# Mixing stage: two projection tiles that follow each other share one buffer of raw weights

## The chip, the cores and the metric

The kernel runs on one core of one Trainium2 chip. The metric is device time in microseconds (us): three runs of the kernel before took 1103.85, 1106.62 and 1107.76 us, and their median, 1106.62, is the time before. The core has five engines that each work through their own instructions in order: TensorE (PE: matmuls; its weight loads are listed apart as PEld), VectorE (DVE), ScalarE (ACT), GpSimd (POOL) and SyncE (SP), which here only issues transfers from device memory. Engines wait for each other and for transfers by semaphores.

## The reference

One step of a hybrid decoder layer on 512 new prompt tokens and 8 sequences of 4 new tokens each, 544 tokens in all, with a model width of 1024. A half-step SwiGLU feed-forward network comes first, then the mixing stage, then a second feed-forward network. What the mixing stage computes, cut down:

```python
proj = h @ w_in                       # h: normed tokens, w_in: 1024 x 3592
q_a, k_a, v_a, q_m, k_m, v_m, o_m, gates = jnp.split(proj, idx, axis=-1)
# 4 heads of differential attention, per query block of 128:
logits = einsum('bqhcd,bkhcd->bchqk', q, k) * ATT_DQ ** -0.5   # c = 2 halves of 64
p = softmax(where(mask, logits + bias, -inf)); a = p[:, 0] - lam * p[:, 1]
attn = a @ v                          # the 8 sequences also attend to paged caches
# 4 heads of chunkwise mLSTM on q_m, k_m, v_m with the gates, and its new states
h_m = rmsnorm(h_m) * sigmoid(o_m)
return concat([attn, h_m]) @ w_out, k_rows, v_a, C, n, m
```

Everything is float32.

## The kernel before, in words

**Matmuls.** The 544 tokens are worked on in two halves of 272 columns. A float32 matrix product is made of three passes over numbers that are rounded to a shorter format (`mm3`, L253 to L255): high weights times high tokens, high weights times low tokens, low weights times high tokens. The tokens are split into high and low once; the weights are split on the chip, tile by tile, in `parts`: ScalarE casts the raw weights to the high part `wh` (L241), and VectorE subtracts that from the raw weights to get the low part `wl` (L242).

**Weights of the mixing stage.** `w_in` without its gates is 28 tiles of 128 columns, each 1024 x 128 float32, 512 KB. A tile is loaded by the sync queue (L226, in `load_raw`) into a raw buffer, [128, 8, 256] float32, and only the first 128 of its 256 columns are used. The raw buffers are two (L854), and the split parts wh and wl have three buffers each (L855). A tile's split is two casts of 128 x 512 and two subtractions. `mix_weights` (L1662) is a generator: each `next` on it issues one tile's load and split. The tiles come in the order 0, 4, 8, 1, 2, 3, 5, 9, 6, 10, 7, 11 (query, key and value of the four attention heads), then 12, 16, 20, 13, ... (the mLSTM heads) and 24 to 27 (output gates). The gates' weights and tiles 0 and 4 are asked for early, at the end of the feed-forward network (`next_h`, L829); the others when `mix` (L1673) projects with them.

**What else runs in the stage.** `mix` interleaves the projections with side work: the gate work of the mLSTM (`gates`, L1091 to L1200: small ScalarE and VectorE instructions in a long chain, some of whose results TensorE needs at L1160 and L1183), attention blocks (`attn_block`, L1298) and the attention to the paged caches (`attn_samples`: gathers on GpSimd's queue, L1360, transposed by TensorE at L1386). An attention head starts with `key_parts` (cs, L1283 and L1284) and `query_parts` (vb, L1293 and L1295): ScalarE casts and VectorE subtracts, and TensorE's logits matmul (L1311) needs both. There is one buffer vb, so the parts of the next query block are made after the logits of this one.

**What sets the order.** All of this is written as Python generators. A tile scheduler then decides, when the kernel is built, the order in which each engine holds its instructions, by program order, by its own estimates of time and by when buffers come free; on the chip that order is fixed. A change in where a load is issued can therefore move instructions of other engines.

Of the kernel before, what the change touches and what calls it, by code (L numbers as in the profile page):

```python
# [10 lines left out]
F32 = mybir.dt.float32  # L11
# [19 lines left out]
H = 4  # L31
# [3 lines left out]
KT = D // 128  # L35
# [170 lines left out]
class _Builder:  # L206
# [1000 lines left out]
        nc.vector.tensor_copy(out=self.ncol, in_=ps[:, 0:NS])  # L1207


    def w_in_tile(self, mt):  # L1210
        win = self.i["w_in"][0].rearrange("(k p) m -> p k m", p=128)
        return self.split(self.load_raw(win[:, :, mt * 128:mt * 128 + 128], 128), KT, 0)

    def proj_half(self, w, hs, dst, half, scale):
        ps = self.acc_tile(half)
# [446 lines left out]
    def mix_weights(self):  # L1662

        yield self.gate_weights()
        for mt in [0, 4, 8, 1, 2, 3] + [4 * a + h for h in range(1, H) for a in (1, 2)]:
            yield self.w_in_tile(mt)
        for h in range(H):
            for a in range(3):
                yield self.w_in_tile(12 + 4 * a + h)
        for h in range(H):  # L1670
            yield self.w_in_tile(24 + h)

    def mix(self, hs, ws, gpost, finish, before):  # L1673
        nc, tc = self.nc, self.tc
# [336 lines left out]
```

## Time and profile before

| what | value |
| --- | --- |
| median of three runs | 1106.62 us |
| span of the profiled execution (its own time; no other is listed for it) | 1109.2 us |
| mixing stage in that span | about 345 to 712 us |
| TensorE busy | 1088.8 us, 98% |
| ScalarE's casts of raw weights (128 x 512 and two other forms) | 165 instructions, 126.8 us |
| VectorE's subtractions for them | 165 instructions, 146.9 us |
| loads of w_in tiles | 28 of 512 KB, 4.8 us (median) from issue to landing |

In the rows of a timeline the columns are the start in us from the start of the span, the duration, the engine, the line, the operation with its tiles (out<-in) and shapes, how many instructions the row holds, and in brackets the idle time of the engine ahead of it and what ended that. A matmul's duration includes time in which the next has started already; the distance between two starts tells the pace. "The granted clock" is the share of full speed that TensorE was given.

### The profile page before, as it was taken

To read this page: it belongs to the slowest core of one execution; us is meant where nothing else is said; L and a number is where in the kernel's file an instruction comes from. 1 tells how busy PE (TensorE), PEld (TensorE's weight loads), DVE (VectorE), ACT (ScalarE), POOL (GpSimd) and SP (SyncE) were. 2 spreads that over 40 slices of the span, in tenths; PEclk is the share of its full clock that TensorE was granted. 3 is DMA by queue.
4 is the path that set the end of the run, shared out by engine and by line. 5 is a ranking of instruction groups with operands and counts; after the bars stand their busy time and mean duration, and the time that the engine had idled before them with its cause. 6 is when DMAs were issued, how large, how long until landed. Compare 5 with 4: busy or idle time off the path is not lost. (4 is left out here: it accounts for less than half of the span.)

```text
span 1109.2 us, 21539 instructions
## 1 busy us (share of the span) xinstructions
PE 1088.8 (98%) x8610; PEld 1050.2 (95%) x8610; DVE 855.4 (77%) x1626; ACT 639.5 (58%) x1288; POOL 163.2 (15%) x212
## 2 busy tenths in 40 slices
PE   9999999999999999999999999999999999999997
PEld 8999999999999998899789888999999999999997
DVE  5898787887677898668666477799978778957865
ACT  6554544565567756666545466675555455555664
POOL 3100000001210424320333442001000000012000
PEclk9999999999999999999999999999999999999999
DMA  9723233237994346533345545864223323299832
GB/s 265 252 94 114 81 111 115 76 96 208 223 245 128 93 121 172 175 112 82 103 148 160 178 136 177 248 216 161 89 87 105 114 77 106 67 270 206 191 97 81
DMA packets 145588, 160.33 MB, mean 145 GB/s; under 512 B 6013, under 2 KB 135397, under 8 KB 144208
## 3 DMA queue, kind: packets, MB, share of 16 engines
q1 hardware_dynamic: 115008, 99.05, 29.5%
q0 software_dynamic: 27472, 57.14, 20.8%
q10 hardware_dynamic: 3008, 2.78, 0.9%
q8 instruction: 67, 1.10, 0.4%
q14 instruction: 33, 0.27, 0.1%
HBM read 143.19 MB, written 16.28 MB: 144 GB/s over the span
## 5 line engine op out<-in xcount | busy, mean ns | idle before, releaser
L241 ACT CAST wh<-raw 128x512 fp32r<-128x512 f32 (+2 forms) x165 | 126.8, 795 | 97.3 <-PE acc L254 34.3
L242 DVE TENSOR_TENSOR wl<-raw,wh 128x512 fp32r<-128x512 f32 (+2 forms) x165 | 146.9, 904 | 43.4 <-ACT wh L241 42.7
L253 PE MATMUL acc<-h,wh 128*128 128x272 f32 x552 | 165.7, 300 | 0.0
L255 PE MATMUL acc<-h,wl 128*128 128x272 f32 x552 | 161.4, 293 | 0.0
L254 PE MATMUL acc<-h,wh 128*128 128x272 f32 x552 | 161.0, 292 | 0.0
L483 PE MATMUL acc<-t,wh 128*128 128x272 f32 x472 | 136.7, 290 | 0.0
L485 PE MATMUL acc<-t,wl 128*128 128x272 f32 x472 | 136.5, 290 | 0.0
L484 PE MATMUL acc<-t,wh 128*128 128x272 f32 x472 | 136.1, 289 | 0.0
L253 PEld LDWEIGHTS acc<-h,wh 128*128 128x128 f32 x552 | 104.9, 190 | 8.1 <-issue 7.5
L255 PEld LDWEIGHTS acc<-h,wl 128*128 128x128 f32 x552 | 104.9, 190 | 0.6 <-issue 0.4
L254 PEld LDWEIGHTS acc<-h,wh 128*128 128x128 f32 x552 | 105.1, 190 | 0.3 <-DVE y L1459 0.2
L483 PE MATMUL acc<-h,wh 128*128 128x272 f32 x360 | 104.2, 290 | 0.0
L485 PE MATMUL acc<-h,wl 128*128 128x272 f32 x360 | 104.2, 289 | 0.0
L484 PE MATMUL acc<-h,wh 128*128 128x272 f32 x360 | 103.6, 288 | 0.0
L242 DVE TENSOR_TENSOR wl<-X,wh 128x1024 fp32r<-128x1024 f32 x66 | 80.7, 1223 | 28.3 <-ACT wh L241 28.3
L241 ACT CAST wh<-X 128x1024 fp32r<-128x1024 f32 x66 | 69.3, 1050 | 40.6 <-PE aux L484 26.0
L484 PEld LDWEIGHTS acc<-t,wh 128*128 128x128 f32 x472 | 89.0, 189 | 0.0
L483 PEld LDWEIGHTS acc<-t,wh 128*128 128x128 f32 x472 | 88.8, 188 | 0.0
L485 PEld LDWEIGHTS acc<-t,wl 128*128 128x128 f32 x472 | 88.7, 188 | 0.1
L732 POOL DMA_DIRECT2D late<-in_ffn_w_down_dram x12 | 18.8, 1563 | 439.4 <-DVE wl L242 241.6
L485 PE MATMUL aux<-h,wl 128*128 128x272 f32 x240 | 69.6, 290 | 0.4 <-DVE wl L242 0.4
L483 PE MATMUL aux<-h,wh 128*128 128x272 f32 x240 | 69.4, 289 | 0.0
(522 smaller groups left out, 3288.6 us busy)
## 6 DMA issues: line engine op xcount, KB each, us to landing
raw<-in_ffn_w_gate_dram SPq DMA_DIRECT2D x18, 1024.0 KB, 5.8
raw<-in_w_in_dram SPq DMA_DIRECT2D x28, 512.0 KB, 4.8
late<-in_ffn_w_down_dram POOLq DMA_DIRECT2D x12, 1024.0 KB
rawx<-in_ffn_w_up_dram SPq DMA_DIRECT2D x10, 1024.0 KB
X<-in_ffn_w_up_dram SPq DMA_DIRECT2D x8, 1024.0 KB, 5.4
raw<-in_ffn_w_down_dram SPq DMA_DIRECT2D x8, 1024.0 KB, 8.6
raw<-in_ffn_w_down_dram SPq DMA_DIRECT2D x10, 768.0 KB, 4.5
raw<-in_w_out_dram SPq DMA_DIRECT2D x7, 1024.0 KB, 5.3
```

The costliest lines, as they stand in the source:

```text
L241: self.nc.scalar.copy(out=high, in_=src)
L242: self.nc.vector.tensor_tensor(out=low, in0=src, in1=high.bitcast(F32), op=ALU.subtract)
L253: nc.tensor.matmul(ps, lhsT=wh, rhs=xh(k0 + k), start=st, stop=False)
L254: nc.tensor.matmul(ps, lhsT=wh, rhs=xl(k0 + k), start=False, stop=False)
L255: self.last_mm = nc.tensor.matmul(ps, lhsT=wl, rhs=xh(k0 + k), start=False, stop=sp).ins
L483: nc.tensor.matmul(ps, lhsT=wh[:, k, cs], rhs=high, start=st, stop=False, skip_group_check=True)
L484: nc.tensor.matmul(ps, lhsT=wh[:, k, cs], rhs=low, start=False, stop=False, skip_group_check=True)
L485: self.last_mm = nc.tensor.matmul(ps, lhsT=wl[:, k, cs], rhs=high, start=False, stop=sp, skip_group_check=True).ins
L732: nc.gpsimd.dma_start(out=ts[j], in_=rows_of(a, j, up), accum_op=ALU.add)
```

## The change

`w_in_tiles` takes the whole order of tiles and goes through it in pairs: (0, 4), (8, 1), (2, 3), (5, 9), (6, 10), (7, 11), (12, 16) and so on to (26, 27). For a pair it takes one raw buffer, issues both loads into its two halves, and then yields the first tile's split and, when it is asked again, the second's. A buffer is free again when both of its tiles are split. The buffers' number and size, each load's size and the splits are as before.

```diff
-    def w_in_tile(self, mt):
+    def w_in_tiles(self, order):
+
         win = self.i["w_in"][0].rearrange("(k p) m -> p k m", p=128)
-        return self.split(self.load_raw(win[:, :, mt * 128:mt * 128 + 128], 128), KT, 0)
+        for i in range(0, len(order), 2):
+            two = order[i:i + 2]
+            raw = self.raw.tile([128, 8, 256], F32, name="raw")
+            for a, mt in enumerate(two):
+                self.nc.sync.dma_start(out=raw[:, :, a * 128:a * 128 + 128], in_=win[:, :, mt * 128:mt * 128 + 128])
+            for a in range(len(two)):
+                yield self.split(raw, KT, a * 128)
...
         yield self.gate_weights()
-        for mt in [0, 4, 8, 1, 2, 3] + [4 * a + h for h in range(1, H) for a in (1, 2)]:
-            yield self.w_in_tile(mt)
-        for h in range(H):
-            for a in range(3):
-                yield self.w_in_tile(12 + 4 * a + h)
-        for h in range(H):
-            yield self.w_in_tile(24 + h)
+        order = [0, 4, 8, 1, 2, 3] + [4 * a + h for h in range(1, H) for a in (1, 2)]
+        order += [12 + 4 * a + h for h in range(H) for a in range(3)]
+        yield from self.w_in_tiles(order + [24 + h for h in range(H)])
```

In the changed kernel the loads are at L1217; the lines of attention are 7 higher (L1293 is L1300, L1311 is L1318), and from `mix` on lines are 3 higher. The instructions are the same in number; the order of the engines differs in a short piece of the program, at about 380 to 445 us of the span before. Three places of it follow.

The sync queue, where the mixing stage's loads begin, before (mixc and setupc are tables of constants):

```order
L226 DMA raw<-in_w_in_dram 128x8x128 x2
L986 DMA mixc<-in_c_mix_dram 128x279
L989 DMA setupc<-in_c_setup_dram 128x962
L226 DMA raw<-in_w_in_dram 128x8x128 x26
```

and with the change:

```order
L1217 DMA raw<-in_w_in_dram 128x8x128 x4
L986 DMA mixc<-in_c_mix_dram 128x279
L989 DMA setupc<-in_c_setup_dram 128x962
L1217 DMA raw<-in_w_in_dram 128x8x128 x24
```

The loads of tiles 8 and 1 now stand ahead of the two tables.

ScalarE from the gate chain (L1026, L1103, L1104) to the logits of the first query blocks (vb: query parts, L1322 or L1329: the softmax's exponentials), before:

```order
L241 CAST wh<-raw 128x512 x2
L1193 ACTIVATE ds_4947<-ds_4947 32x128
L1196 COPY ds<-ds_4947 32x128
L1283 CAST cs<-k 64x512 x2
L1293 CAST vb<-X_3965 64x128 x4
L241 CAST wh<-raw 128x512 x4
L1293 CAST vb<-X_3965 64x128
L1322 ACTIVATE L,z<-L,z 128x128
L1293 CAST vb<-X_3965 64x128 x2
L1322 ACTIVATE L,z<-L,z 128x128
L1293 CAST vb<-X_3965 64x128 x5
L1322 ACTIVATE L,z<-L,z 128x256
```

and with the change:

```order
L241 CAST wh<-raw 128x512 x2
L1193 ACTIVATE ds_4946<-ds_4946 32x128
L1196 COPY ds<-ds_4946 32x128
L1290 CAST cs<-k 64x512 x2
L1300 CAST vb<-X_3965 64x128 x4
L241 CAST wh<-raw 128x512 x2
L1300 CAST vb<-X_3965 64x128 x4
L1329 ACTIVATE L,z<-L,z 128x128 x2
L1300 CAST vb<-X_3965 64x128 x4
L1329 ACTIVATE L,z<-L,z 128x256 x2
```

Between the query parts of the first and the second block stand two casts of raw weights (one tile) instead of four; each tile's casts stand one tile earlier, the first ones ahead of L1103.

TensorE, from the logits of the first query block (128 wide) to those of the second (256 wide), before:

```order
L1311 MATMUL aux<-cs,vb 128x128 x4
L253 MATMUL acc<-h_4200,wh 128x272
L254 MATMUL acc<-h_4201,wh 128x272
L255 MATMUL acc<-h_4200,wl 128x272
...
L1311 MATMUL aux<-cs,vb 128x256
L253 MATMUL acc<-h_4200,wh 128x272
L1311 MATMUL aux<-cs,vb 128x256
L254 MATMUL acc<-h_4201,wh 128x272
L255 MATMUL acc<-h_4200,wl 128x272
L253 MATMUL acc<-h_4200,wh 128x272
L1311 MATMUL aux<-cs,vb 128x256 x2
```

and with the change:

```order
L1318 MATMUL aux<-cs,vb 128x128 x4
L253 MATMUL acc<-h_4200,wh 128x272
L254 MATMUL acc<-h_4201,wh 128x272
L255 MATMUL acc<-h_4200,wl 128x272
L253 MATMUL acc<-h_4200,wh 128x272
L254 MATMUL acc<-h_4201,wh 128x272
L1318 MATMUL aux<-cs,vb 128x256
L255 MATMUL acc<-h_4200,wl 128x272
L253 MATMUL acc<-h_4200,wh 128x272
L254 MATMUL acc<-h_4201,wh 128x272
L1318 MATMUL aux<-cs,vb 128x256
L255 MATMUL acc<-h_4200,wl 128x272
```

Before, twelve projection matmuls stand between the two groups (three are shown) and the 256-wide ones come close together; now five stand there, and the 256-wide ones are spread among projection matmuls.

## The prediction

> **What bounds the kernel now.** I read the page first, then the waits of TensorE in the mixing stage, then the raw tile's own view, and last the timelines of TensorE and ScalarE around the one place that these name.
>
> ```profile
> span 1109.2 us, 21539 instructions
> PE 1088.8 (98%) x8610; PEld 1050.2 (95%) x8610; DVE 855.4 (77%) x1626; ACT 639.5 (58%) x1288; POOL 163.2 (15%) x212
> ```
>
> TensorE is busy 98% of the span and carries the time. The change touches only when raw weights arrive, so it can gain only where TensorE waits, through another engine, for such a load, or where its clock suffers from such a wait. The next fence holds three views: waits of TensorE from 396 to 437 us, the same for ScalarE (one row), and the raw tile from 437 to 640 us. Columns of a wait are total us, times and longest us.
>
> ```profile
> PE aux L1311 <- ACT wh L241: 1.5, 1, 1.5
> PE aux L1311 <- ACT vb L1293: 0.2, 1, 0.2
> ...
> ACT wh L241 <- DMA raw<-in_w_in_dram: 2.5, 3, 1.2
> ...
> L226 SPq DMA_DIRECT2D raw<-in_w_in_dram x18: 367/368/368, 440.0 to 617.2; - x18
>   PE acc L254: 22.5, 12
> DMA to landing us min/median/max: 3.8/4.9/6.6
> ```
>
> The casts of raw weights (L241) wait for a load three times, 2.5 us together, all before 437 us. After that, 18 more loads are issued and no cast waits for one: the casts wait for TensorE to give a weight buffer back (22.5 us, 12 times). There a load that comes sooner changes nothing. Of the three early waits only one is seen on TensorE. ScalarE and TensorE around it:
>
> ```profile
> 404.77 1.14 ACT L241 CAST wh<-raw 128x512 fp32r<-128x512 f32 x2 [0.43 <-DMA raw<-in_w_in_dram]
> 412.44 1.15 ACT L241 CAST wh<-raw 128x512 fp32r<-128x512 f32 x2 [4.64 <-PE acc L254]
> 413.61 0.66 ACT L1144 ACTIVATE ce<-m 4x544 f32<-4x544 f32 x1
> 417.63 1.14 ACT L241 CAST wh<-raw 128x512 fp32r<-128x512 f32 x2 [0.91 <-DMA raw<-in_w_in_dram]
> 424.52 1.26 ACT L1293 CAST vb<-X 64x128 fp32r<-64x128 f32 x4
> 425.80 1.14 ACT L241 CAST wh<-raw 128x512 fp32r<-128x512 f32 x2
> 428.13 1.14 ACT L241 CAST wh<-raw 128x512 fp32r<-128x512 f32 x2 [1.19 <-DMA raw<-in_w_in_dram]
> 429.18 0.29 ACT L1293 CAST vb<-X 64x128 fp32r<-64x128 f32 x1
> 431.04 0.30 ACT L1293 CAST vb<-X 64x128 fp32r<-64x128 f32 x1
> ```
>
> ```profile
> 426.10 0.56 PE L1311 MATMUL aux<-cs,vb 128*128 128x128 f32 x3
> 428.31 0.29 PE L254 MATMUL acc<-h,wh 128*128 128x272 f32 x1
> 428.43 0.29 PE L255 MATMUL acc<-h,wl 128*128 128x272 f32 x1
> 430.23 0.39 PE L1311 MATMUL aux<-cs,vb 128*128 128x256 f32 x1 [1.51 <-ACT wh L241]
> 430.95 0.28 PE L253 MATMUL acc<-h,wh 128*128 128x272 f32 x1
> 431.39 0.53 PE L1311 MATMUL aux<-cs,vb 128*128 128x256 f32 x2 [0.15 <-ACT vb L1293]
> 432.17 0.43 PE L253 MATMUL acc<-h,wh 128*128 128x272 f32 x1
> 432.40 0.43 PE L254 MATMUL acc<-h,wh 128*128 128x272 f32 x1
> 436.24 0.37 PE L253 MATMUL acc<-h,wh 128*128 128x272 f32 x1
> ```
>
> ScalarE works in order. At 428.13 its cast of tile 6 has waited 1.19 us for the load; queued behind it are the casts of the second query block (vb, L1293, 429.18 to 431.34), and TensorE's logits matmul (L1311) needs those. Two matmuls start 0.12 us apart when nothing is late (428.31 and 428.43), but from 428.43 to 430.23 pass 1.80 us, so 1.68 are lost, and from 430.95 to 431.39 another 0.44 − 0.12 = 0.32. Together 2.0 us.
>
> There is more behind it. These are stretches of the span in the view by windows: length, busy us of TensorE, its weight loads, VectorE, ScalarE, GpSimd, then the granted clock, DMA share and GB/s.
>
> ```profile
> 428.33:431.74 3.41, 1.75 (x13) 1.31 (x12) 2.31 (x9) 2.92 (x10) 1.77 (x3) 1.00 0.79 203
> 431.74:435.16 3.42, 3.42 (x17) 3.32 (x16) 3.20 (x15) 2.33 (x8) 0.21 (x1) 0.50 0.61 189
> 564.86:568.27 3.41, 1.65 (x14) 1.45 (x13) 1.90 (x9) 1.04 (x5) 0.44 (x2) 1.00 0.50 150
> 568.27:571.69 3.42, 3.42 (x18) 3.42 (x17) 0.65 (x3) 0.96 (x4) 0.28 (x1) 0.50 0.06 19
> ```
>
> Twice TensorE is busy only about half of a stretch of 3.41 us (1.75 and 1.65), and both times the next stretch of the same length runs at a granted clock of 0.50. The stall by the late load is followed by a slow stretch, in which matmuls start 0.23 us apart (432.17, 432.40) instead of 0.12.
>
> **The change part by part.** *Same work.* 28 loads of 512 KB, the same casts, subtractions and matmuls are issued before and after; nothing is added or removed, cost 0. What moves is when loads go out, and with them the order in which ScalarE, VectorE and TensorE stand.
>
> *When loads go out.* The sync queue waits for a raw buffer at nearly every load, and the buffer is free when VectorE has subtracted (L242):
>
> ```profile
> SPq L226 <- DVE wl L242: 239.4, 26, 24.4
> ...
> 407.91 0.37 SPq L226 DMA_DIRECT2D raw<-in_w_in_dram  x1
> ...
> 420.65 0.37 SPq L226 DMA_DIRECT2D raw<-in_w_in_dram  x1
> ...
> 422.84 0.37 SPq L226 DMA_DIRECT2D raw<-in_w_in_dram  x1
> ```
>
> Before, a load goes out when the tile two places ahead is split. After, both loads of a pair go out when the second tile of the pair before the last is split: that is three places ahead for a pair's first tile and four for its second. So no load goes out later than before, and a pair's second goes out two tiles sooner. By the order of the tiles, the release at 407.91 (which brought tile 3) now brings 5 and 9; the release at 420.65 (tile 9) now brings 6 and 10. Tile 6 thus leaves at 420.65 instead of 422.84, 2.19 us sooner, and 3 is there long before 412.44, where its cast waited for it (the row names TensorE, but its load had gone out at 407.91 and loads take 3.8 to 6.6 us, so it cannot have been there before 411.7).
>
> *How long two loads take together.* No row shows a pair of w_in loads with these sizes in one buffer. Bounds from the page:
>
> ```profile
> raw<-in_w_in_dram SPq DMA_DIRECT2D x28, 512.0 KB, 4.8
> raw<-in_ffn_w_gate_dram SPq DMA_DIRECT2D x18, 1024.0 KB, 5.8
> raw<-in_ffn_w_down_dram SPq DMA_DIRECT2D x8, 1024.0 KB, 8.6
> ```
>
> From below 4.8 us (the second load does not slow the first), from above 8.6 us (the slowest 1 MB row). I take 5.8: also 1 MB into one such buffer through the same queue. Tile 6 then lands at 420.65 + 5.8 = 426.45 (425.45 to 429.25) instead of about 428.1.
>
> *The wait on TensorE.* ScalarE ends the first block's casts at 425.78. Tile 9's cast (425.80 before) now stands earlier, before L1193, so tile 6's cast starts at about 426.5 and ends at 427.6, and the vb casts of block two, which now follow in one run of four, take 1.26 us from there: 427.6 to 428.9 instead of 429.18 to 431.34. TensorE's order has the 256-wide L1311 matmuls earlier and spread between projection matmuls, the first five rows behind the 128-wide ones, so it asks for the first piece at about 426.10 + 0.75 (four of them, by 0.56 for three) + 5 × 0.12 = 427.5 and for the others until 429. VectorE also does tile 9's subtraction before the first block's parts now, for which I count 0.3 us of idle ahead of that. The first piece needs two of the four casts, half of 1.26: 428.2, that is 0.4 us after 427.5 + 0.3; the later pieces another 0.3 by estimate. So 2.0 us of idle become 1.0 (0.3 + 0.4 + 0.3): **−1.0 us**. Bounds: 0 (tile 6 lands at 429.25, later than now) and −2.0 (nothing left).
>
> *The clock.* If TensorE idles 1.0 us instead of 2.0 in that stretch, in three pieces, the slow stretch should go. Its worth: 3.42 us at 0.12/0.23 of the normal pace lose at most 3.42 × (1 − 0.12/0.23) = 1.64 us; some rows in it are small matmuls that lose less, so 1.4. In this execution that makes −1.0 − 1.4 = −2.4: the row at 436.24 would stand at 433.8, and the span would be 1106.8. In another execution the stretches need not begin at the same place: a stall of 1.68 us falls wholly into one stretch of 3.41 in (3.41 − 1.68)/3.41 = 0.51 of the positions. So a median execution loses between 0.7 and 1.4 to the clock, and I take **−1.1**, with 0 and −1.64 as bounds.
>
> *The gate chain.* Tile 3's cast stands ahead of L1103 now and pushes the small gate work by at most its half, 0.6 us; L1144 ended at 414.27, and TensorE wants it in this row, with no wait shown:
>
> ```profile
> 415.50 0.47 PE L1160 MATMUL aux<-base,ce 36*128 36x36 f32 x5
> 434.91 0.21 POOL L1782 COPY qz<-X 64x32 f32<-64x32 f32 x1 [4.46 <-DMA pgin<-in_cache_k_dram,idx]
> 444.99 1.04 PE L1386 MATMUL smp<-base,pgin 128*128 128x128 f32 x8
> ```
>
> Slack is 415.50 − 414.27 = 1.2 us, so cost 0; without that cover it is 0.6. Page gathers on GpSimd's queue now run beside pairs: a copy waits for one until 434.91, but TensorE reaches that batch of pages first at 444.99, 10 us later. Cost 0 up to 10 us of delay.
>
> Sum for the median: 1106.62 − 1.0 − 1.1 = **1104.5 us**. The profiled execution lies 2.6 us above the median of the three (1103.85 to 1107.76); its own sum is 1109.2 − 2.4.
>
> **The rivals.** *B, the stall moves* (the loads were not the limit): the weight buffers wh and wl are three deep, and TensorE's releases hold the later casts (22.5 us in 12 waits). If tile 6's cast waits for such a release too, or TensorE meets as much idle at the new places of L1311, which ask for the casts sooner, the waits and the slow stretch remain; a change that doesn't bring the loads sooner ends here as well. Against it: tile 6's wait at 428.13 is put to the load, and in the row ahead of it a cast (425.80) shows no wait at all. Price: 0 to −1.0, so 1106.2.
>
> *E, the slow stretch stays*: it does not hang on this stall. For it: only two cases in the span tie half clock to idle, and neither stretch before it was wholly idle (1.75 and 1.65 busy). Against it: in both the slow one follows at once. Then the gain is that of the waits alone: 1106.6 − 1.0 = 1105.6. The Trainium skill ("TensorE: Matmul & The Clock Gate", Part 1: The HAM clock gate) says the same: half clock comes after a whole idle window of some 3.4 us, so a stall of 1.7 would not bring it. The two cases in the trace disagree with that rule.
>
> *C, more than the sum*: the whole 2.0 us of idle go, with 1.64 of the clock, and the other slow stretch (568.27) goes too, because all behind has shifted against the stretches, another 1.4. 1106.6 − 2.0 − 1.6 − 1.4 = 1101.6, and with half of the last 1102.3. Against it: the idle before 568.27 has nothing to do with raw loads.
>
> *D, slower*: two loads together land late. Tile 5 shares its landing with 9; its load leaves at 407.91, and its cast stands before L1144 on ScalarE. Landing by the 8.6 row at 416.5, the cast ends at 417.65 and L1144 at 418.3 instead of 414.27: 4.0 late, 1.2 covered, so TensorE loses 2.8 at L1160, and an idle like that brings a slow stretch of 1.4. The same landing time puts tile 6 at 429.25, so nothing is gained at L1311: 1106.6 + 4.2 = 1110.8. It decides from a landing of about 7.5 us: then the idle at L1160 is 1.7, as long as the stall that went, and tile 6 is no sooner than now. Against it: 5.8 is the nearer row, and there only 0.1 us is not covered.
>
> **How the numbers follow.** 0.56 for the forecast, 0.12 for B, 0.10 for E, 0.12 for C, 0.10 for D. 0.3% is 3.3 us, about what a measurement can tell from no change: faster means below 1103.3, slower above 1109.9. Of the forecast a quarter lies below 1103.3 (runs of one kernel spread by 2 us to each side) and 3% above 1109.9; of B and E 3% and 5%; of C nine tenths below; of D about two thirds above. Faster 0.26, slower 0.09, same 0.65. Range 1101.5 to 1108.0: C's lower half and most of D are left out; the forecast's own range is 1102.5 to 1106.5.
>
> **What would show it.** In the changed profile: no wait of L241 on a w_in load before 437 us; the wait of 1.51 us on the logits matmul gone, with single waits under 0.5; no stretch at clock 0.50 between 425 and 440; tiles 5 and 9 issued together near 408, 6 and 10 near 420.7; no wait at L1160. Wrong would be: a wait on DMA still there, a slow stretch behind a shorter stall, a new wait at L1160 or L1183, or a time above 1108.

## The result, and the profile after

The changed kernel takes 1107.85 us (median of 22 runs, 1105.15 to 1111.96), the kernel before 1105.91 us in the same comparison (22 runs, 1102.54 to 1110.44): a ratio on record of 1.0026, 95% interval 1.0017 to 1.0035 (the two medians alone give 1.0018). That is slower by a little under the 0.3% that the prediction called no change, and against the forecast of 1104.5 us. The range (1101.5 to 1108.0) holds the time.

The profiled execution of the changed kernel looks otherwise. Its page, and the waits of ScalarE from 396 to 437 us:

```profile
span 1106.5 us, 21535 instructions
PE 1087.5 (98%) x8610; PEld 1048.4 (95%) x8610; DVE 855.2 (77%) x1626; ACT 639.3 (58%) x1288; POOL 164.7 (15%) x212
```

```profile
ACT wh L241 <- PE acc L254: 8.4, 4, 4.2
```

Its span is 2.7 us below that of the profiled execution before. No cast of raw weights waits for a load any more: all their idle time up to 437 us (8.4 us, four times) ends with TensorE giving back a weight buffer. In the same stretch TensorE's own waits, and then the sync queue, ScalarE and TensorE in order of time:

```profile
PE aux L1318 <- DVE vb L1302: 0.4, 2, 0.3
```

```profile
409.05 1.30 SPq L1217 DMA_DIRECT2D raw<-in_w_in_dram  x2
421.74 0.99 SPq L1217 DMA_DIRECT2D raw<-in_w_in_dram  x2
```

```profile
407.05 1.14 ACT L241 CAST wh<-raw 128x512 fp32r<-128x512 f32 x2 [1.57 <-PE acc L254]
408.10 0.65 ACT L1103 ACTIVATE e<-e 4x544 f32<-4x544 f32 x1
...
425.61 1.26 ACT L1300 CAST vb<-X 64x128 fp32r<-64x128 f32 x4
427.32 1.14 ACT L241 CAST wh<-raw 128x512 fp32r<-128x512 f32 x2 [0.44 <-PE acc L254]
428.76 1.26 ACT L1300 CAST vb<-X 64x128 fp32r<-64x128 f32 x4 [0.31 <-PE aux L1318]
```

```profile
427.72 0.44 PE L1318 MATMUL aux<-cs,vb 128*128 128x128 f32 x2 [0.25 <-DVE vb L1302]
428.34 0.33 PE L1318 MATMUL aux<-cs,vb 128*128 128x128 f32 x1 [0.18 <-DVE vb L1302]
428.50 0.34 PE L253 MATMUL acc<-h,wh 128*128 128x272 f32 x1
...
429.05 0.29 PE L254 MATMUL acc<-h,wh 128*128 128x272 f32 x1
429.43 0.39 PE L1318 MATMUL aux<-cs,vb 128*128 128x256 f32 x1
429.66 0.28 PE L255 MATMUL acc<-h,wl 128*128 128x272 f32 x1
```

This is the step of the prediction, nearly to the number: the loads of a pair leave together, tile 6's cast stands behind the first block's parts and waits only for TensorE, the parts of block two are cast in one run, and the first 256-wide logits matmul starts 0.38 us after the matmul ahead of it (429.05 to 429.43), where 1.80 us passed before. In the view by windows (columns as in the prediction) the stretch of the stall and the next one are now:

```profile
427.67:431.08 3.41, 3.08 (x19) 2.55 (x19) 3.26 (x14) 2.85 (x10) 2.50 (x4) 1.00 0.72 200
431.08:434.49 3.41, 3.41 (x25) 2.90 (x23) 3.29 (x16) 2.75 (x9) 0.83 (x2) 1.00 1.05 315
```

TensorE is busy 3.08 of 3.41 us instead of 1.75, and the slow stretch is gone. To compare traces further I take the time between two fixed matmuls of TensorE's order (8610 in both kernels, equal in order but for the few shown). From the 3261st to the 3331st, which I call the logits piece (423.5 to 436.5 us before), pass 12.99 us before and 10.73 after: −2.26, where −2.4 was forecast. From there on the two profiled executions differ by other things. So the place was right in this pair of traces and the time of the kernel was wrong: the experiments ask whether the gain is there in other executions, whether the first comparison holds, and where the rest goes.

### The profile page after: what moved, and what is told of

Its sections match the earlier page's. It is cut to its first block, busy times and chain, and to the rows that moved or that the text cites. A ratio compares the mean times of both kernels' runs of the same rounds, so it can differ in the third digit from the quotient of the medians.

```text
span 1106.5 us, 21535 instructions
## 1 busy us (share of the span) xinstructions
PE 1087.5 (98%) x8610; PEld 1048.4 (95%) x8610; DVE 855.2 (77%) x1626; ACT 639.3 (58%) x1288; POOL 164.7 (15%) x212
## 4 chain that ended last, share of the span: by engine, by line
PE 89%; DVE 5%; ACT 3%; DMA 2%; issue 1%; POOL 0%; POOLq 0%; DVEq 0%; ACTq 0%
PE acc L485 9%; PE acc L483 9%; PE acc L484 9%; PE acc L253 8%; PE acc L255 7%; PE acc L254 7%; PE aux L485 5%; PE aux L483 5%; PE aux L484 5%; PE smp L485 2%; PE smp L483 2%; PE smp L484 2%; PE smp L1393 1%; PE acc L747 1%; PE acc L746 1%; PE acc L745 1%
```

## Experiments

**Timed again.** The changed kernel went through five more sessions, in each against the kernel before, which twice also ran under another name against itself. Edits: none.

> The changed kernel as it stands, timed against the one before on the chip of this call. On the first chip the ratio was 1.0026; on the chip of the two partial kernels the one before was slower (1109.37 us) and both partial kernels faster than it. Theory A (the change costs something steady that the first comparison saw): 1.002 to 1.003 here too. Theory B (the early gain of 1.0 to 2.3 us is steady, and what else differs is the lot of transfers and of the clock, which falls differently in each session): between 0.998 and 1.000 here, so a sign other than the first.

> The changed kernel timed once more, in another session. So far its ratio to before was 1.0026 (first chip) and 1.0006 (a later one). Theory A (a steady cost of about 0.2%): 1.001 to 1.003. Theory B (no steady cost; the traces' early gain, other transfers' and the clock's lot beside it, a sign that changes with the session): anywhere from 0.997 to 1.003, and the control of this call, the same kernel against itself, departs from 1 as far.

> The kernel before against itself, the same file under another name, in the same call: what the comparison says when nothing is changed. Theory A: 1.0000 within its interval, so a ratio of 1.0026 elsewhere means something. Theory B: it can lie 0.1 to 0.2% off 1.

> The changed kernel in a further session, above all for one more trace. In the traces so far the first 100 matmuls take 16.9 to 17.2 us in every kernel with the change's order (five traces) and 15.95 to 16.9 in the others. The piece depends on where the first change of the clock to full speed falls: at 4.8 to 5.3 us in three of three traces of before, at 6.7 to 7.3 us, or at 4.4 with a slow stretch behind it, in four of four of the changed kernel. Theory C (this place belongs to the kernel, so the change pays about 0.9 us there each time): 16.9 us or more here again. Theory B (chance): any value from 15.9 to 17.2. The logits piece, 10.7 to 11.2 by both.

> The kernel before against itself once more, in the same call as the changed one. Theory C: the first 100 matmuls take 16.1 to 16.2 us again, with full clock from 5.0 to 5.3 us on. Theory B: any value from 15.9 to 17.2. The logits piece 11.8, or 13.0 with a slow stretch. Ratio within 0.1% of 1.

> The changed kernel timed in one more session. Ratios so far: 1.0026 (first comparison), 1.0006, 0.9988, 1.0002; the kernel before against itself gave 0.9995 and 1.0008. In the traces the logits piece is steadily 1.0 us shorter (six of six), and pieces behind it give some of it back (page transposes up to 0.9 us, the piece from 610 to 634 us 0.3 us, the one from 521 to 554 us 0.3 us). Theory B (net gain of a few tenths of a us, lost in a scatter of 2 us): 0.998 to 1.001, and the mean of the sessions behind the first is below or at 1. Theory A (a steady cost of 0.26%, as the first comparison has it): 1.002 to 1.003.

> The changed kernel timed in a further session. Four later sessions gave 1.0006, 0.9988, 1.0002 and 1.0001, the first comparison 1.0026, where the kernel before had a median of 1105.91 us against 1109.05 to 1109.37 in all later ones. Theory A2 (the cost of 0.26% is real where the kernel before runs that fast, on that chip): if before comes out near 1106 us here, the ratio is 1.002 to 1.003; where before is near 1109 us, the ratio is 0.999 to 1.001. Theory B (the first comparison is an outlier of its session): 0.999 to 1.001 whatever the level of before.

| run | this, median us | before, median us | ratio | 95% interval |
| --- | --- | --- | --- | --- |
| first comparison | 1107.85 | 1105.91 | 1.0026 | 1.0017 to 1.0035 |
| after_timed | 1110.29 | 1109.18 | 1.0006 | 0.9990 to 1.0021 |
| after_timed2 | 1108.18 | 1109.31 | 0.9988 | 0.9973 to 1.0004 |
| after_timed3 | 1108.07 | 1109.06 | 1.0002 | 0.9988 to 1.0016 |
| after_timed4 | 1109.70 | 1109.05 | 1.0001 | 0.9983 to 1.0019 |
| after_timed5 | 1107.83 | 1108.20 | 0.9996 | 0.9983 to 1.0009 |
| before_control | 1108.23 | 1109.31 | 0.9995 | 0.9983 to 1.0007 |
| before_control2 | 1109.46 | 1109.06 | 1.0008 | 0.9995 to 1.0021 |

The mean of the five later ratios is 0.9999, and they scatter by 0.0007: no change that can be measured, a few tenths of a us at most. The control is as far from 1 as the changed kernel is. What sets the first comparison apart is the kernel before, which was 2.3 to 3.5 us faster there than in all six later sessions (with that of the partial kernels below: 1108.20 to 1109.37 us); the changed kernel's 1107.85 lies among its later medians. No later session had before at 1106, so whether the loss of 0.26% belongs to the session of that comparison, or is real where the kernel before runs so fast, stays open. A steady cost of 0.26% (theory A) is not there in the other five.

**A second trace of each.**

> The kernel before once more, for a second trace. The profiled execution of before lay at a span of 1109.2 us, while its runs have a median of 1105.91 us; the changed kernel's runs are 1.8 to 3.3 us longer than their spans. If that holds for before too, its typical span is about 1104 and the profiled one was slow by some 5 us: then this trace should lack one or both of the stretches at clock 0.50 and have a span of 1102 to 1106. If the profiled one was typical, both slow stretches are here again and the span is 1108 to 1110.

> The changed kernel once more, for a second trace. If the wait of 1.9 us for a page gather at 559.7 us is a steady effect of the paired loads (theory 1), it is here again, at 1 us or more. If it is chance, it is missing and the span is below 1105.

The kernel before took 1110.63 us with a span of 1108.6, the changed one 1107.95 us with 1106.2. Neither side of the expectation came out clean: both slow stretches are missing in before, and yet its span is almost that of the first profile. The same stall is there, shorter:

```profile
428.74 1.14 ACT L241 CAST wh<-raw 128x512 fp32r<-128x512 f32 x2 [0.85 <-DMA raw<-in_w_in_dram]
429.79 0.29 ACT L1293 CAST vb<-X 64x128 fp32r<-64x128 f32 x1
```

```profile
429.40 0.29 PE L255 MATMUL acc<-h,wl 128*128 128x272 f32 x1
430.84 0.39 PE L1311 MATMUL aux<-cs,vb 128*128 128x256 f32 x1 [1.16 <-ACT vb L1293]
```

These two fences are of the kernel before's second trace. The logits piece takes 11.77 us there, without a slow stretch, and 10.72 in the second trace of the changed kernel: the gain without the clock is 1.05 us. In the changed kernel the wait for a page gather, 1.9 us at 559.7 in the first trace, is missing at that place in the second (its wait of 0.6 us is at a later gather): not a steady effect, though the span, 1106.2, is not below the 1105 that I had set for that case.

**Early pairs alone, late pairs alone.** In `w_in_tiles` of the changed kernel, the pairs for the first twelve tiles only (early_pairs):

```diff
-        for i in range(0, len(order), 2):
-            two = order[i:i + 2]
+        for two in [order[i:i + 2] for i in range(0, 12, 2)] + [[mt] for mt in order[12:]]:
```

and for the last sixteen only (late_pairs):

```diff
-        for i in range(0, len(order), 2):
-            two = order[i:i + 2]
+        for two in [[mt] for mt in order[:12]] + [order[i:i + 2] for i in range(12, len(order), 2)]:
```

> Pairs for the first twelve tiles only (0 to 11 in the attention heads' order), the sixteen later tiles one by one, each in a buffer of its own. The order of instructions on every engine is that of the change. Theory 1 (the loss comes from the later pairs: 1 MB at once beside the page gathers, so that TensorE waits for a gather as at 559.7 us in the changed kernel): here the loss is gone and the early gain is left, ratio 0.997 to 1.000. Theory 2 (the loss comes from the new order and loads between 380 and 445 us, and the profile of before was not typical): the whole loss is here, ratio about 1.003.

> The first twelve tiles one by one as before, the sixteen later ones in pairs. The order of instructions on every engine is that of the kernel before; only the moments at which the later loads go out differ. Theory 1 (later pairs delay gathers): ratio 1.003 to 1.005, with a wait of TensorE for a page gather (L1456's place) of 1 to 3 us. Theory 2 (the early part): ratio 0.999 to 1.001, no such wait more often than before.

early_pairs: 1107.87 us, ratio 0.9985 (0.9974 to 0.9997); late_pairs: 1107.91 us, 0.9979 (0.9964 to 0.9993), against 1109.37 for before. Neither loses. The late pairs do not cost in time what theory 1 said; and theory 2 falls too, since the early pairs have the change's order on every engine and no loss. One half of theory 1 did come: in the trace of late_pairs TensorE waits 1.94 us for the page gather at 560.25, the same place as in the first trace of the change. That wait is in two of the eight traces with late pairs and in none of the eight without, too few to call it theirs. That late_pairs comes out 0.2% faster, with before's order and nothing to gain where its casts never waited, suggests how far such a ratio can be off; the controls were off by 0.05 and 0.08%. The traces are plainer: the logits piece takes 11.02 us with early pairs, and 12.95 (with a slow stretch) with late pairs.

**One pair, three pairs.** Which of the early pairs does it? Three kernels that ran once each, for their traces (1109.81, 1111.80 and 1109.92 us): the same place with only some pairs, for one_pair the one that starts at position 6 of the order (first_three has 0, 2 and 4 there, next_three 6, 8 and 10):

```diff
-        for i in range(0, len(order), 2):
-            two = order[i:i + 2]
+        for two in [order[j:j + n] for i in range(0, len(order), 2)
+                    for j, n in ([(i, 2)] if i in (6,) else [(i, 1), (i + 1, 1)])]:
```

> Only tiles 5 and 9 share a buffer and are loaded together; all others as before. This frees tile 6's load one tile sooner (about 420.7 instead of 422.8 us). Instructions move only around the logits of the second query block, ahead of L1103 nothing moves. If the stall at L1311 hangs on tile 6's load, the piece of TensorE's order from its first 128-wide L1311 to the 256-wide row behind (13.0 us with a slow stretch, 11.8 without, in the kernel before) takes 10.7 to 11.0 us here, as in the changed kernel. If it hangs on the earlier pairs, it stays at 11.8 to 13.0.

> Only the first three pairs (0 and 4, 8 and 1, 2 and 3); all others one by one as before. TensorE's order is that of before; on ScalarE and VectorE only places around the gate chain move. If the stall at L1311 hangs on tile 6's load, it is here as in before: the same piece takes 11.8 us, or 13.0 with a slow stretch. If the gate chain is pushed by the cast that stands ahead of L1103 now, TensorE waits at L1160 or L1183 by up to 0.6 us.

> Only the pairs 5 and 9, 6 and 10, 7 and 11 share buffers; 0 to 3 and 8 one by one, and all from 12 on too. Instructions are ordered as with the one pair 5 and 9. There the cast of tile 9, which stands ahead of L1193 now, waited 3.69 us for its load (issued at 413.47, beside tile 5's), and the logits piece took 13.0 us. If the early pairs are what brings tile 9's load in time, the cast waits here too and the piece takes 11.7 us or more; if the pairs around tile 6 are enough, it takes 10.7 to 11.2.

| kernel | logits piece, us | slow stretch in it |
| --- | --- | --- |
| before, four traces | 12.99, 11.77, 11.78, 11.74 | in the first |
| late_pairs | 12.95 | yes |
| first_three | 11.88 | no |
| one_pair | 13.00 | yes |
| next_three | 14.20 | yes, two |
| early_pairs | 11.02 | no |
| the change, seven traces | 10.73, 10.72, 11.18, 10.73, 10.72, 11.09, 11.03 | none |

The first three pairs alone leave the stall. But tile 6's load alone does not cure it either, as I had expected of one_pair: it makes it worse. ScalarE and TensorE in one_pair:

```profile
422.36 1.14 ACT L241 CAST wh<-raw 128x512 fp32r<-128x512 f32 x2 [3.69 <-DMA raw<-in_w_in_dram]
423.41 0.31 ACT L1193 ACTIVATE ds<-ds 32x128 f32<-32x128 f32 x1
...
426.38 1.26 ACT L1300 CAST vb<-X 64x128 fp32r<-64x128 f32 x4
```

```profile
425.78 0.29 PE L255 MATMUL acc<-h,wl 128*128 128x272 f32 x1
427.11 0.30 PE L1318 MATMUL aux<-cs,vb 128*128 128x128 f32 x1 [1.03 <-ACT vb L1300]
428.27 0.44 PE L1318 MATMUL aux<-cs,vb 128*128 128x128 f32 x2 [0.87 <-DVE vb L1302]
```

The order moves tile 9's cast ahead of L1193, as in the changed kernel, but its load leaves as the second of the pair that goes out at 413.47, lands only at 422.3, and the cast waits 3.69 us for it. All that is behind on ScalarE is late, the first block's parts included, and TensorE stalls at its 128-wide logits. next_three does the same (its cast at 422.27 waits 3.65 us). In the changed kernel the first three pairs bring that pair of loads to 409.05, and the same place has no wait for a load. So the early gain came only where both were there: the new order and tile 9's load in time. The prediction had named only tile 6's.

The load was not only sent later. From issue to landing it took 8.4 us in one_pair and in next_three, and 5.4 to 5.9 in the changed kernel and early_pairs. With 5.4 us it would, by estimate, have landed at 419.3 (it left 0.4 us behind 413.47), only 0.6 us after ScalarE began to wait for it, so most of the wait is that slow landing, and why it was slow in these two kernels is open. Whether the order and tile 6's load would have been enough without it, these runs do not show.

first_three also answers the gate chain: TensorE's order from its 3021st to its 3201st matmul, with L1160 in it, takes 23.45 us as in all others.

**Where the gain goes.** The pieces behind, from the same traces, in us; before's order are the four traces of before, late_pairs and first_three, the change's order its seven traces and early_pairs:

| piece of TensorE's order (us in before) | before's order | the change's order | difference of the means |
| --- | --- | --- | --- |
| 3261 to 3331 (423 to 436), logits | 11.74 to 12.99 | 10.72 to 11.18 | −1.28 |
| 3431 to 3481 (448 to 454) | 6.35 in all | 6.35 to 6.45 in five, 7.07 to 7.16 in three | +0.30 |
| 4201 to 4266 (545 to 555) | 9.85 to 10.06 in four, 10.59 and 10.77 | 9.71 and 9.93, 10.61 to 10.77 in six | +0.26 |
| 4851 to 4901 (629 to 635) | 6.32 in all | 6.60 in all | +0.28 |
| 5201 to 5291 (670 to 682) | 11.59 to 13.28 | 11.51 to 12.50 | −0.45 |

Three pieces give back 0.84 of the 1.28 on the mean. By the scatter of the traces (standard errors) the −1.28 is uncertain by 0.26, the +0.30 by 0.13 and the +0.26 by 0.21. One is exact, 0.28 us in eight of eight: in the changed kernel

```profile
630.75 0.66 PE L1393 MATMUL smp<-base,pgin 128*128 128x128 f32 x4 [0.28 <-ACT pgT L1394]
```

a page transpose waits for ScalarE's copy of the one before it, which in before_control starts without a wait:

```profile
629.07 0.66 PE L1386 MATMUL smp<-base,pgin 128*128 128x128 f32 x4
629.56 0.39 PE L1531 MATMUL aux<-vt,L 128*128 128x130 f32 x2
```

The copy itself starts 0.28 us later against TensorE. Its rows in the changed kernel and in before_control:

```profile
630.11 0.58 ACT L1394 COPY pgT<-smp 128x512 f32<-128x512 f32 x1 [4.86 <-PE aux L1530]
```

```profile
628.43 0.59 ACT L1387 COPY pgT<-smp 128x512 f32<-128x512 f32 x1 [4.58 <-PE smp L1386]
```

In before_control it goes as soon as its transposes are done, in the changed kernel only behind two matmuls that follow them (L1523, now L1530), although each engine's order is the same there. This does not hang on TensorE being early: one_pair and next_three, with logits pieces of 13.0 and 14.2 us, have the same wait and 6.60 us, while late_pairs and first_three have 6.32. So it belongs to the kernels with the new order around the second block's logits, 200 us ahead of it. Why the copy's wait moved, no run shows.

The first of the three, in after_timed and, where it is absent, in after_timed2:

```profile
449.78 1.14 ACT L241 CAST wh<-raw 128x512 fp32r<-128x512 f32 x2 [4.12 <-PE aux L1252]
...
451.42 0.57 ACT L1394 COPY pgT<-smp 128x512 f32<-128x512 f32 x1
```

```profile
452.04 0.66 PE L1393 MATMUL smp<-base,pgin 128*128 128x128 f32 x4 [0.82 <-issue]
```

```profile
448.88 1.14 ACT L241 CAST wh<-raw 128x512 fp32r<-128x512 f32 x2 [3.40 <-PE acc L254]
...
450.52 0.56 ACT L1394 COPY pgT<-smp 128x512 f32<-128x512 f32 x1
```

A cast starts 0.9 us later (0.7 against TensorE, whose matmuls are 0.17 us later there), behind it the copy of a page, and TensorE's next transpose waits 0.8. The cast does not wait for a load here; it goes after another matmul of TensorE, and why it does so in three of eight traces, and in none of one_pair, next_three and before's order, is open. The second is a wait of 0.8 us on ScalarE's copy of a softmax row, seen in after_timed:

```profile
PE aux L1538 <- ACT aT L1346: 0.8, 1, 0.8
```

It occurs in before's order too (two of six traces), only less often. Whether that difference is more than chance, these traces cannot say.

What is left of −1.28 is −0.44 us, or −0.9 with the last row, whose swings are mostly waits for a page gather, of 0.1 to 1.4 us in seven of the fourteen traces. Pieces with larger swings (the start, the value gathers at 558 to 566, the second network at 985) move the total of a single execution by 2 us either way. Five sessions put the whole at −0.2 us with an uncertainty of about 0.3 (0.9999, scatter 0.0007 over five). The −0.44 agrees with that, the −0.9 only roughly.

A third raw buffer, which would bring loads sooner without sharing, was not tried. Only two of the partial kernels were timed over several runs, and not beside the whole change, so nothing here says that one of them is better than it.

## Why the prediction was right or wrong

- **What bounds, and which wait reaches TensorE:** right, but not complete. The three waits on w_in loads before 437 us are gone, the later casts wait for weight buffers, and the stall at the logits goes. It goes with the new order and tile 9's load as well as with tile 6's: the kernels with the order and the sooner load of tile 6 alone had tile 9 late and kept a stall. The pieces from 2901 to 3261 are equal to 0.02 us in the traces of both orders.
- **The wait on TensorE, −1.0:** right in size. Without the clock 11.77 (mean of 11.77, 11.78, 11.74) against 10.72 to 11.18 in the changed kernel: −1.04 to −0.58, −0.88 on the mean. The two ends of the sum were both too high: TensorE's idle time in the piece goes from 1.5 to 1.6 us (without the slow stretch) to 0.5 to 0.7, where I had 2.0 and 1.0.
- **Two loads together, 5.8 us:** too long for the first of a pair. The raw tile's view from 340 to 460 us has, for the changed kernel and for one_pair,

```profile
DMA to landing us min/median/max: 3.9/5.2/8.8
```

```profile
DMA to landing us min/median/max: 4.0/4.5/8.4
```

  and by the transfers' own records in the changed kernel the first of the pairs (5, 9) and (6, 10) lands after 4.0 to 5.0 us, the second after 5.3 to 6.3 (some of these records are incomplete). The row of 5.8 fits the pair, not its first tile, so tile 6 had more room than I gave it. The 8.4 of one_pair is tile 9, close to my upper bound of 8.6.
- **The clock, −1.1:** mis-sized. The stall brought a slow stretch in the logits piece in two of six traces with before's order, worth 1.2 us each time (12.99 or 12.95 against 11.76): −0.4 on the mean. I had read one execution, where it occurs, and weighed the stall's position in a stretch at 0.5 to 1; and I started from a profiled span of 1109.2 as if it were typical of 1106.62.
- **Everything behind at nothing:** this is the step that failed, with the clock. I carried the gain of one place to the end of the span unreduced and priced nothing behind it but waits for page gathers. The pieces at 448, 545 and 629 give back 0.84 us on the mean, and not by gathers: TensorE waits there for work that ScalarE does. Only the 0.28 us at 629 is certain, in ten of ten traces with the new order around the logits; the other two come in some traces, and their cause is open. With −0.88 for the wait and −0.4 for the clock, −0.44 is left of the −2.1 of the sum.
- **The gate chain, 0:** right. The cast ahead of L1103 pushes it (L1103 at 408.10 instead of 406.44, of which 1.15 us are TensorE's own later place in this execution, so by 0.5 us, as in all eight traces with the change's order), and L1160 shows no wait. The 0.6 that I had allowed was covered.
- **Rivals.** B, the stall moves: not at the logits, where tile 6's cast waits 0.44 us for a weight buffer and the idle time is less than half of what it was; some idle time is new at the three places behind. E, the stretch stays: no. D, slower because a pair lands late: not in the changed kernel, but one_pair and next_three show that very mechanism at tile 9, a landing after 8.4 us, a cast that waits 3.7 us and a logits piece of 13.0 and 14.2 us.
- **The time:** measured slower by 0.26% in the comparison on record, and unchanged in five others. Nothing in the traces explains +2 us, and the cause of that one comparison stays open. That 1107.85 lies inside the stated range says little for the sum, since the range reached 1.4 us above the 1106.62 of the kernel before; I had given a slower result 0.09 and no change 0.65.

## What to carry to other kernels

Before counting the gain of a stall to the end of the span, compare the time between fixed instructions over the whole program: here a change of order around 430 us went with a wait of 0.28 us at 630, at a place whose own order had not moved, and the kernels with the order but without the gain had it too. One profiled execution tells where a wait is, not how often it occurs: with a scatter of 2 us between executions, a second and third trace of the unchanged kernel cost less than a wrong sum. And a change of a tenth of a per cent needs a control: the same file against itself differed by up to 0.08% here, and one session of the change stood 0.27% off the mean of the five others.

## What the runs showed of the hardware

**Half clock came after stretches that were only half idle, but not after all of them.** The granted clock changes only at the borders of stretches of 3.41 us. In the sixteen traces, between the start and the end of the kernel, 13 stretches have TensorE busy for less than 1.9 us; eight of them are followed by half clock, five are not. Of the stretches with 1.9 us or more one is, in next_three, a stretch of 3.26 us at half clock itself. The start and the end are different: there half clock also followed busy times of 3.27 us (first_three, from 7.40 us) and 2.20 us (before_control2, from 1094.93 us), so the busy time of this profile alone does not decide it. Two that differ, of late_pairs and of the changed kernel, at the same place of the program:

```profile
557.73:561.14 3.41, 1.47 (x8) 0.14 (x2) 1.23 (x4) 1.08 (x6) 1.97 (x3) 0.99 0.29 77
561.14:564.55 3.41, 3.41 (x16) 3.22 (x16) 0.90 (x4) 0.17 (x1) 1.84 (x2) 0.51 0.59 186
```

```profile
557.37:560.79 3.42, 1.52 (x9) 0.24 (x3) 1.10 (x3) 0.96 (x6) 2.10 (x3) 1.00 0.39 98
560.79:564.20 3.41, 3.41 (x28) 3.41 (x29) 1.15 (x5) 1.13 (x5) 1.71 (x2) 1.00 0.80 191
```

1.47 brings half clock and 1.52 does not, while 1.75 did in the kernel before. The Trainium skill ("TensorE: Matmul & The Clock Gate", Part 1: The HAM clock gate) has a whole idle window of about 3.4 us as the condition; the length agrees with the traces, the condition does not.

**The start of a kernel took up to 1.3 us more or less, by where the stretches fell.** The first 100 matmuls take 15.9 to 17.2 us in the traces. By the clock records of the traces, with full clock granted from 4.50 us on they take 15.90, from 5.12 on 16.17, from 6.63 on 16.90 and from 7.23 on 17.18; in the three traces with 3.99, 4.08 and 4.44 a half-clock stretch follows at about 11 us, and they take 16.9 to 17.1. I had taken the difference between the first traces for the change's doing; after_timed3 (16.29) and before_control2 (16.63) showed that it is not.

**Two engines start late together, and no row names a cause.** In after_timed, ScalarE's cast (449.78) and VectorE's next instruction (449.82) start 0.6 to 0.7 us later against TensorE than in after_timed2 (448.88 and 449.01), while the matmuls themselves go at the same pace.
